# Layer 1's attention entry with its casts shared over three engines, wide matmuls of ones at the kernel's entry, and a moved order in layer 0's attention

## The chip, the cores and the metric

The kernel runs on one core of a Trainium2 chip. A core has a matrix engine (TensorE, PE in the profile; its weight loads are listed apart as PEld), three engines that work on tiles element by element (VectorE or DVE, ScalarE or ACT, GpSimd or POOL) and a queue that issues most transfers (SyncE or SP). Each engine runs its own instructions strictly in order and waits for others by semaphores. The metric is the device time of one execution in microseconds, and the number to predict is its median over the runs.

## The reference, cut to what matters

The model has two layers over 1024 tokens of width 1024, all in float32. Layer 0 mixes tokens by differential attention (8 heads), layer 1 by latent attention (16 heads) with a rotary key that all heads share. Each is followed by a gated MLP with a short convolution.

```python
# layer 1's attention (mla_attention)
proj = h @ w_in
c_q = rms_norm(proj[..., :384], q_norm_g)
c_kv = rms_norm(proj[..., 384:640], kv_norm_g)
k_pe = apply_rope(proj[..., 640:], cos, sin)          # one rotary key of 32 for all heads
q = (c_q @ w_uq).reshape(b, s, 16, 64 + 32)
kv = (c_kv @ w_ukv).reshape(b, s, 16, 64 + 64)
sc = (einsum('bqhd,bkhd->bhqk', qn, k_nope) + einsum('bqhr,bkr->bhqk', qp, k_pe)) * scale
p = masked_softmax(sc, mask)                          # chunk-causal
o = einsum('bhqk,bkhe->bqhe', p, v)
```

## The kernel before, in words

Products run in a rounded float32 format. To keep float32 accuracy, an operand is split into a high part (a cast, helper `hi`, L123 to L127) and a low part (the difference, helper `lo`, L129), and a product is made of three matmuls (`mm3`, L116 to L121: high by low, high by high, low by high). So every tile that enters a product costs one cast, on ACT unless the call names DVE, and one subtraction, on DVE unless the call names POOL. PSUM, where products land, is divided into two big tiles S of 1024 columns, three banks b and one bank u of 512.

**The entry** (`diff_attention`, from L373). Rows of x are loaded, squared on ACT (L157), scaled by the root on DVE (norm, L440), transposed on PE (L448), cast and subtracted, and then multiplied by the first weights. The order on PE, DVE, ACT and POOL is written out by hand in the string `FIRST` (L366). In it T are the transposes of a row tile, H and L its casts and low parts, Q, R and N the squares, the root and the norm, G the copy of the gains out of PSUM, p the products of the first weights, and z0 to z3 runs of `spin` (L191): matmuls of a tile of ones that nobody reads. Their counts are 0, 28, 0 and 6, each 128 columns wide.

**Layer 0's attention** runs in steps of two blocks of queries, four steps to a head. What each step emits on the four engines is written by hand in `DA_SCORE` (L324), one row for each step of a head, and `DA_SECOND` for the very second step. Tokens without a mark belong to the current step, one more apostrophe is one step older, a plus one step ahead. S are scores on PE, M the maximum on DVE, E the exponential on ACT, I the inverse sum on DVE, C the scaling (POOL in a head's first two steps), X the mixing of the two maps on DVE, T transposes on PE, H and L their cast and low part, A the product with the values, O the copy of the output. Q, R, N and F finish a head's half: Q3 is a low part of the squares on POOL, F (L1947, L1948) adds them up on PE. U and V are the next projections (0 and 1 on PE), W the next weight's cast (h, ACT) and low part (l, POOL). Engines take only their own tokens, so two neighbouring tokens of different engines may change places without any change to an engine's order.

**Layer 1's attention** (`mla_input` L1526, `mla_heads` L1650) isn't ordered by hand. Instructions are emitted in program order, and a planner with its own estimates of their lengths places them on the engines. While `mla_input` still makes the latents, the first steps of the attention start (`early`). A head has four steps t, and a step scores two blocks of queries (L1977 to L1991: products into S, maximum on DVE, exponential on ACT). Beside them, `prepare(t)` and `units(t)` (L1749 on) feed the next pair of heads:

- `rotary` (L1737) writes the rotary key into head 0's key tile, 32 rows by ACT and 32 by DVE; `share(j, half)` (L1744) copies it into the key tiles of heads 1 to 3, casts of 64x1024 on ACT. Heads 2 and 3 get theirs in steps 3 to 6.
- `split_w(p)` and `split_v(p)` cast the weights and the values of a pair on ACT and subtract on POOL.
- `q_unit` makes half a head's queries: nine matmuls, a multiplication by the table on DVE (L1694), a cast on ACT, a low part on DVE for heads 0 and 1 and on POOL after.
- `k_unit` makes half a pair's keys: six matmuls, two casts of 64x512 on ACT, two low parts on DVE.
- The six units of pair 1 are due in steps 2, 3, 4, 5, 6 and 7.

Of the kernel before, what the change touches and what calls it, by code (L numbers as in the profile page):

```python
# [10 lines left out]
F32 = mybir.dt.float32  # L11
F32R = mybir.dt.float32r
# [6 lines left out]
P = 128  # L19
S = 1024  # L20
# [36 lines left out]
class Trunk:  # L57
# [133 lines left out]
    def spin(self, n):  # L191

        ps = self.bank("u")
        for _ in range(n):
            self.nc.tensor.matmul(ps[:, :P], self.ones, self.ones, start=True, stop=True)

    def gain(self, place, src):
        g = self.at(place, [P, src.shape[-1]])
# [4 lines left out]
    def constants(self):  # L203
        nc, a = self.nc, self.a
        c = lambda name, shape, dt=F32: self.const.tile(shape, dt, name=name, tag=name)
        self.ident = c("ident", [P, P])
        make_identity(nc, self.ident)
        self.row = self.at("u13", [8, P])
        nc.scalar.dma_start(self.row, a["attn_norm_g"][0:1, :].rearrange("o (k p) -> (o k) p", p=P))
        nc.scalar.preload_act_table_set("natural_log_exp_and_others")  # L210
        self.mhalf = c("mhalf", [P, 1])
        nc.gpsimd.memset(self.mhalf, -0.5)
        self.eps = c("eps", [P, 1])
        nc.gpsimd.memset(self.eps, EPS)
        self.ones = c("ones", [P, P], F32R)
        nc.vector.tensor_scalar(self.ones, self.ident, 0.0, 1.0, ALU.mult, ALU.add)
        self.conv = [c(f"conv{l}", [P, 2 * NF, 4]) for l in range(2)]
        self.g_sub = c("g_sub", [P, 1])
        self.neglam = c("neglam", [P, 1])
# [69 lines left out]
    def steps(self, attend, units, prepare, n, apart=False):  # L289
# [32 lines left out]


    DA_SCORE = (  # L324
# [4 lines left out]
    )  # L329

    DA_SECOND = "S0 I1' Vc' Ukd' T3'' H2'' M0 L2'' A1'' C0' X0' H3'' E0b L3'' Wh U0 A2'' E0a Vt' N3'''' A3'' C1' O'' Wl' X1' Q2'' I0 U1 C0 S1 X0 Us Vh' Q1'' T0' H0' Q3'' Up F'' Um M1 Ua Wl R1'' Vl' E1b V0 E1a L0' I1 A0' R2'' R3'' Uqa Uqd Uqe Uqb C1 X1 N1'' Uqc V1 T1 T0 Uqf H0"

    DA_END = (
# [9 lines left out]
    def da_steps(self, attend, units, prepare, n, extra):  # L343
# [4 lines left out]
        with self.tc.manual_schedule(engines={E.PE, E.DVE, E.Activation, E.Pool}):  # L348
            for t in range(-1, first + len(self.DA_END)):
                while len(steps) < min(n, t + 2):  # L350
# [3 lines left out]
                    for name, u in zip("UV", units(x)):  # L354
                        steps[x].parts.update({name + part: f for part, f in u.items()})
                row = self.DA_SECOND if t == 1 else self.DA_SCORE[t % 4] if t < first else self.DA_END[t - first]
                for name in row.split():
# [15 lines left out]
    def diff_attention(self, o_d, project):  # L373
        nc, a = self.nc, self.a
# [6 lines left out]
            k=self.ring("u0", "u1", "u2"), qh=self.ring("u3", "u4"), v=self.ring("u5", "u6", "u7"),  # L381
            P=self.ring("u8", "u9", "u10", "u11", "u12"), pT=self.ring("u13", "u14", "u15"),
# [11 lines left out]
        def fetch_w(h, which):  # L394
            if h < DA_HEADS:
                raws[h, which] = self.fetch(a["da_wqkv"][h, which], D)
# [24 lines left out]
        x, r = [], {}  # L421
# [10 lines left out]
        def fetch_tab(half):  # L432
            s = slice(half * 512, half * 512 + 512)
            nc.sync.dma_start(tab[:, :, s], a["rope_da"][:, :, s])
# [82 lines left out]
            next(ends[which], None)  # L517

        todo = dict(c=column, g=spreads, G=keep, t1=lambda: fetch_tab(1), f1=lambda: fetch_w(1, 1), s=self.load_constants)
        for i, n in enumerate((0, 28, 0, 6)):  # L520
            todo[f"z{i}"] = lambda n=n: self.spin(n)
        for i in range(NT):
            todo.update({f"{z}{i}": lambda f=f, i=i: f(i) for z, f in zip("QRNX", (squares, root, norm, fetch_x))})
# [1002 lines left out]
    def mla_input(self, W, hts, turns, v_d, heads_of):  # L1526
# [120 lines left out]
                heads.early()  # L1647
        return heads

    def mla_heads(self, cT, v_d, o_d):  # L1650
        nc, a = self.nc, self.a
        pairs = MLA_HEADS // 2
        heads = [dict() for _ in range(MLA_HEADS)]
        W, V, raws = {}, {}, {}
        w_places = [("u2", "u3"), ("u4", "u5")]
        v_ring, q_ring, t_ring = self.ring("s13", "s4"), self.ring("s1", "s11", "s5", "s9"), self.ring("h10", "h11", "h8")
        k_places, kT = ["s0", "s10", "s12", "s8"], []
# [3 lines left out]
            P=self.ring("u12", "u6", "u7", "u8", "u9"), pT=self.ring("u0", "u1", "u10", "u11"), o=self.ring("h4", "h5", "h6", "h7"),  # L1661
        )

        def fetch_w(p):
            raws["w"] = self.fetch(a["mla_w"][p], D)

        def split_w(p):
            raw = raws["w"]
            W[p] = [self.at(x, [P, D], F32R) for x in (w_places[p % 2] if p else self.cut("s9"))]
            self.hi(W[p][0], raw)  # L1670
            self.lo(W[p][1], raw, W[p][0], nc.gpsimd)

        def fetch_v(p):
# [2 lines left out]
        def split_v(p):  # L1676
            rv = raws["v"].rearrange("p (k h e) -> p k h e", h=2, e=64)
            V[p] = v = v_ring([P, NT, 2, 2, 64], F32R)
            self.hi(v[:, :, :, 0, :], rv)
            self.lo(v[:, :, :, 1, :], rv, v[:, :, :, 0, :], nc.gpsimd)  # L1680

        def q_unit(h, half):
            if half == 0:
                heads[h]["q"] = q_ring([P, 2, S], F32R)
            q = heads[h]["q"]
            acc = self.bank()
            off = (h % 2) * 384
            for k in range(3):
                wh, wl = (w[:, off + k * P : off + (k + 1) * P] for w in W[h // 2])
                self.mm3(acc, wh, wl, cT.q(0, half, k), cT.q(1, half, k), k == 0, k == 2)  # L1690
            yield
            s = slice(half * 512, (half + 1) * 512)
            t = t_ring([P, 512])
            nc.vector.tensor_mul(t, acc, cs[:, s])  # L1694
            self.hi(q[:, 0, s], t)
            self.lo(q[:, 1, s], t, q[:, 0, s], nc.gpsimd if h > 1 else None)

        def k_unit(p, half):
            acc = self.bank()
            for k in range(2):  # L1700
                wh, wl = (w[:, 768 + k * P : 768 + (k + 1) * P] for w in W[p])
                self.mm3(acc, wh, wl, cT.kv(0, half, k), cT.kv(1, half, k), k == 0, k == 1)
            yield
            s = slice(half * 512, (half + 1) * 512)
            for j in range(2):
                k = heads[2 * p + j]["k"] = kT[(2 * p + j) % 4]
                src = acc[j * 64 : j * 64 + 64]
                self.hi(k[0:64, 0, s], src)
                self.lo(k[0:64, 1, s], src, k[0:64, 0, s])

        def pair_units(p):
            return [
                lambda: k_unit(p, 0), lambda: k_unit(p, 1),
                lambda: q_unit(2 * p, 0), lambda: q_unit(2 * p, 1),
                lambda: q_unit(2 * p + 1, 0), lambda: q_unit(2 * p + 1, 1),
            ]

        fetch_w(0)
        split_w(0)

        def first(*which):
# [12 lines left out]
        def k_tiles(n):  # L1734
            kT.extend(self.at(place, [P, 2, S], F32R) for place in k_places[len(kT) : n])

        def rotary(half, t):  # L1737

            k_tiles(1)
            s = slice(half * 512, (half + 1) * 512)  # L1740
            for x, r0 in enumerate((64, 96)):
                self.hi(kT[0][r0 : r0 + 32, :, s], t, nc.vector if x else None)

        def share(j, half):  # L1744
            k_tiles(j + 1)
            s = slice(half * 512, (half + 1) * 512)
            self.hi(kT[j][64:128, :, s], kT[0][64:128, :, s])

        def prepare(t):  # L1749
            p, u = divmod(t, 8)  # L1750
            if t == 0:
                fetch_w(1)
            if t == 1:
                split_w(1)
                k_tiles(4)
            if 3 <= t < 7:
                share(2 + (t - 3) // 2, (t - 3) % 2)
            for at, ahead, f in ((2, 1, fetch_v), (4, 1, split_v), (5, 2, fetch_w), (7, 2, split_w)):
                if u == at and p + ahead < pairs:
                    f(p + ahead)  # L1760
            if t >= 4 * MLA_HEADS - 10:
                prefetch[0]()

        def units(t):
            p, u = divmod(t, 8)
            if t == 0:
                return [u() for u in pair_units(0)[1::2]]

            at = (2, 3, 4, 5, 6, 7) if p == 0 else (0, 1, 3, 4, 5, 7)
            return [pair_units(p + 1)[i]() for i in range(6) if at[i] == u and p + 1 < pairs]  # L1770

        def attend(t):
# [533 lines left out]
```

## Time and profile before

| | |
|---|---|
| median of 3 runs | 2388.96 us (2388.56 to 2390.82) |
| the profiled execution | 2391.28 us, of which 2389.5 us are the profile's span |
| mean granted TensorE clock | 0.997 |
| HBM traffic | 158.85 MB read, 52.43 MB written, 88 GB/s over the span |
| DMA share in the first fortieth of the span | 0.4 of 16 engines |

The profile is that of one execution. Times count in microseconds from the span's start. A row of the order of time has start, length, engine, line, operation and tiles (out<-in), shapes and count, and in brackets the idle time of the engine before it and what ended it. A group's row has the count, the busy time, the mean of one in ns, and the idle time before. Matmuls overlap in a pipeline, so the length of one row is longer than the pace at which they follow each other.

### The profile page before, as it was taken

How to read it: one execution, taken by the hardware profiler on the slowest of the kernel's cores; microseconds unless marked ns; L12 is line 12 of the kernel's file. 1: busy time of each engine (PE TensorE's matmuls, PEld its weight loads, DVE VectorE, ACT ScalarE, POOL GpSimd, SP SyncE). 2: the span in 40 equal slices, each digit the busy share in tenths (PEclk: the TensorE clock that was granted, in tenths of full speed). 3: DMA queues.
4: the chain of work that ended last, by engine and by line, in shares of the span. 5: the costliest groups of instructions: out<-in, count | busy, mean ns of one | idle time of the engine just before them, and what ended most of it. 6: DMA issues, size and time to landing. Idle time of an engine off the chain costs nothing.

```text
span 2389.5 us, 32702 instructions
## 1 busy us (share of the span) xinstructions
PE 2351.9 (98%) x11979; PEld 2003.0 (84%) x11979; DVE 1926.9 (81%) x3180; ACT 1291.6 (54%) x2367; POOL 611.2 (26%) x485
## 2 busy tenths in 40 slices
PE   9999999999999999999999999999999999999998
PEld 8888888888888888888898889988888888887886
DVE  6788888758888888899854778886488888888997
ACT  5677777745444444354445777775354444443544
POOL 4555555324000000000132666664320000000001
PEclk9999999999999999999999999999999999999999
DMA  4111111332222222642221211123322222227502
GB/s 147 40 36 36 48 37 54 111 114 102 89 89 80 80 86 82 233 168 90 86 95 56 63 38 41 41 95 107 115 71 90 87 80 80 89 80 282 176 1 79
DMA packets 95664, 213.39 MB, mean 89 GB/s; under 512 B 8712, under 2 KB 33936, under 8 KB 95504
## 3 DMA queue, kind: packets, MB, share of 16 engines
q1 hardware_dynamic: 86304, 183.51, 23.3%
q10 hardware_dynamic: 9200, 27.80, 3.1%
q8 instruction: 94, 1.54, 0.3%
q14 instruction: 66, 0.54, 0.1%
HBM read 158.85 MB, written 52.43 MB: 88 GB/s over the span
## 4 chain that ended last, share of the span: by engine, by line
PE 86%; DVE 6%; ACT 2%; DMA 2%; POOL 2%; issue 2%; SPq 0%; POOLq 0%; DVEq 0%; ACTq 0%
PE S L119 13%; PE S L121 13%; PE S L120 13%; PE b L119 8%; PE b L121 8%; PE b L120 8%; PE u L119 4%; PE u L121 4%; PE u L120 4%; PE b L260 2%; PE u L2012 1%; PE u L2011 1%; PE S L1856 1%; PE S L1855 1%; PE b L1902 1%
## 5 line engine op out<-in xcount | busy, mean ns | idle before, releaser
L167 POOL TENSOR_TENSOR st<-st,mhalf 128x1 f32<-128x1 f32 x56 | 35.5, 634 | 1305.4 <-DVE st L164 1301.4
L119 PE MATMUL S<-s,u 128*128 128x512 f32 (+1 forms) x800 | 302.1, 378 | 2.4 <-DVE s L130 2.0
L121 PE MATMUL S<-s,u 128*128 128x512 f32 (+1 forms) x800 | 301.1, 376 | 0.4 <-DVE u L130 0.4
L120 PE MATMUL S<-s,u 128*128 128x512 f32 (+1 forms) x800 | 301.0, 376 | 0.0
L127 ACT CAST u<-h 128x512 fp32r<-128x512 f32 (+2 forms) x242 | 145.5, 618 | 272.9 <-DVE h L1023 271.4
L119 PE MATMUL b<-s,u 128*128 128x512 f32 x588 | 230.9, 393 | 2.0 <-DVE u L130 1.4
L121 PE MATMUL b<-s,u 128*128 128x512 f32 x588 | 229.0, 390 | 0.0
L120 PE MATMUL b<-s,u 128*128 128x512 f32 x588 | 229.0, 390 | 0.0
L1080 DVE SCALAR_TENSOR_TENSOR u<-u,conv,u 128x1023 f32<-128x1023 f32 (+1 forms) x176 | 225.0, 1278 | 0.8 <-ACT u L1076 0.7
L149 POOL TENSOR_TENSOR u<-u,st 128x512 f32<-128x512 f32 (+7 forms) x160 | 169.0, 1066 | 164.9 <-DVE st L1997 103.7
L127 ACT CAST s<-u 128x512 fp32r<-128x512 f32 (+3 forms) x230 | 145.4, 665 | 94.8 <-PE u L121 27.1
L119 PEld LDWEIGHTS S<-s,u 128*128 128x128 f32 x800 | 150.5, 188 | 30.7 <-DVE s L130 2.6
L130 DVE TENSOR_TENSOR u<-b,u 128x512 fp32r<-128x512 f32 (+1 forms) x256 | 158.8, 631 | 20.7 <-ACT u L127 18.2
L127 ACT CAST u<-b 128x512 fp32r<-128x512 f32 (+1 forms) x256 | 135.0, 547 | 74.9 <-PE b L1902 42.2
L121 PEld LDWEIGHTS S<-s,u 128*128 128x128 f32 x800 | 150.5, 188 | 28.1 <-DVE u L130 0.6
L120 PEld LDWEIGHTS S<-s,u 128*128 128x128 f32 x800 | 150.5, 188 | 27.4
L119 PE MATMUL u<-s,s 128*128 128x512 f32 (+1 forms) x408 | 162.4, 398 | 1.4 <-DVE h L602 0.6
L121 PE MATMUL u<-s,s 128*128 128x512 f32 (+1 forms) x408 | 158.0, 387 | 0.0
L120 PE MATMUL u<-s,s 128*128 128x512 f32 (+1 forms) x408 | 157.6, 386 | 0.0
L130 DVE TENSOR_TENSOR s<-u,s 128x512 fp32r<-128x512 f32 (+2 forms) x204 | 139.0, 714 | 11.9 <-ACT s L127 11.6
L1083 ACT ACTIVATE u<-u 128x1024 f32<-128x1024 f32 x44 | 46.7, 1062 | 187.2 <-DVE u L1080 187.2
L130 DVE TENSOR_TENSOR u<-h,u 128x512 fp32r<-128x512 f32 x171 | 117.5, 687 | 32.5 <-ACT u L127 31.5
(289 smaller groups left out, 6533.4 us busy)
## 6 DMA issues: line engine op xcount, KB each, us to landing
u<-in_ffn_up SPq DMA_DIRECT2D x88, 512.0 KB, 3.8
g_d<-u ACTq DMA_DIRECT2D x44, 512.0 KB, 2.6
u<-in_ffn_down SPq DMA_DIRECT2D x66, 256.0 KB, 4.7
u<-g_d SPq DMA_DIRECT2D x62, 256.0 KB, 4.3
s<-in_da_wqkv SPq DMA_DIRECT2D x23, 512.0 KB, 3.8
x_d<-u SPq DMA_DIRECT2D x16, 512.0 KB, 2.9
s<-x_d SPq DMA_DIRECT2D x8, 1024.0 KB, 9.9
u<-o_d SPq DMA_DIRECT2D x24, 256.0 KB, 2.9
```

The lines of the kernel that those rows point to most:

```text
L119: mm(out, lh, rl, start=first, stop=False, skip_group_check=onto)
L120: mm(out, lh, rh, start=False, stop=False, skip_group_check=onto)
L121: mm(out, ll, rh, start=False, stop=last, skip_group_check=onto)
L127: self.nc.scalar.copy(out, src)
L130: (eng or self.nc.vector).tensor_sub(out, src, hi.bitcast(F32))
L149: self.nc.gpsimd.tensor_mul(x, x, s.to_broadcast(list(x.shape)))
L167: nc.gpsimd.tensor_tensor(r, s, self.mhalf, ALU.pow)
L260: self.nc.tensor.transpose(ps[:, j * P : (j + 1) * P], probs[t][:, k : k + P], self.ident)
L1080: nc.vector.scalar_tensor_tensor(t[half][:, back:], u[half][:, : S - back], w, t[half][:, back:], ALU.mult, ALU.add)
L1083: nc.scalar.activation(t[0], t[0], AF.Silu)
L1855: nc.tensor.matmul(sc[c][:, b : b + m], ql[c][:, qs], kt[:, c, :m], start=True, stop=False)
L1856: nc.tensor.matmul(sc[c][:, b : b + m], qh[:, c, qs], kt[:, c, :m], start=False, stop=True)
```

## The change

Three places change.

1. `spin` multiplies the ones by a tile `wide` of 512 columns, which four ACT copies of the 128x128 ones fill at the start. The counts fall from 28 to 7 and from 6 to 2.
2. Tokens move in `DA_SCORE` and `DA_SECOND`. Per engine: T3 of the step before goes from behind the next row's S0 to the end of row 0 on PE, and T2 goes ahead of V1; on ACT E0b goes ahead of H1 and E0a behind it in row 0, E0a ahead of Wh in row 1, and Uqa ahead of R2; on DVE M0 goes ahead of Ukd, I0 ahead of X1, and N1 ahead of X1 at the end of the row; on POOL Wl goes ahead of C1. The two tokens moved in row 2 and the two in row 3 belong to different engines.
3. Engines of layer 1's entry are spelled out by letters (S for ACT, V for DVE, P for POOL). Against before, these differ: to DVE go the casts of weight pair 1, of value pair 2, of the shares (2, second half) and (3, first half), of query half 3 and of key piece 3; to POOL go the low parts of query halves 1 and 2, and to DVE that of query half 6. The share (3, first half) is emitted in step 10 in place of 5. The units of pair 1 are due in steps 2, 2, 3, 5, 5 and 7.

```diff
-            self.nc.tensor.matmul(ps[:, :P], self.ones, self.ones, start=True, stop=True)
+            self.nc.tensor.matmul(ps, self.ones, self.wide, start=True, stop=True)
...
+        self.wide = self.at("h4", [P, 512], F32R)
+        for j in range(4):
+            nc.scalar.copy(self.wide[:, j * P : (j + 1) * P], self.ones.bitcast(F32))
...
     DA_SCORE = (
-        "S0 S1 M0 Up O'' R2''' X1' R3''' V0 N1''' M1 T1' Ua E0a H1' L1' Uka E1a T0' H0' Ukb V1 Ukc E0b T2' L0' I0 E1b A0' N2'''",
-        "S0 I1' Vc' Ukd' T3'' H2'' M0 L2'' A1'' C0' X0' H3'' E0b L3'' Wh U0 A2'' E0a Vt' N3'''' A3'' C1' O'' Wl' X1' Q2'' I0 U1 C0 S1 X0 Us Vh' Wl Q1'' T0' H0' Q3'' Up F'' Um M1 Ua R1'' Vl' E1b V0 E1a L0' I1 A0' R2'' R3'' Uqa Uqd Uqe Uqb C1 X1 N1'' Uqc V1 T1 T0 Uqf H0",
+        "S0 S1 M0 Up O'' R2''' V0 X1' R3''' E0b N1''' M1 T1' Ua H1' E0a L1' Uka E1a T0' H0' T2' Ukb Ukc L0' I0 E1b V1 A0' N2''' T3'",
+        "S0 I1' Vc' H2'' M0 Ukd' L2'' A1'' C0' X0' H3'' E0b L3'' U0 E0a A2'' Wh Vt' N3'''' A3'' O'' Wl' Q2'' C1' I0 X1' U1 C0 S1 X0 Us Vh' Wl Q1'' T0' H0' Q3'' Up F'' Um M1 Ua R1'' Vl' E1b V0 E1a L0' I1 A0' Uqa R2'' R3'' Uqd Uqb C1 N1'' Uqe X1 Uqc V1 T1 T0 Uqf H0",
...
-        for i, n in enumerate((0, 28, 0, 6)):
+        for i, n in enumerate((0, 7, 0, 2)):
...
+    SHARES = "SSSVVS"
+    SHARED_AT = (3, 4, 10, 6)
+    ROTARY = "SV"
+    VALUES = "SSVSSSSS"
+    WEIGHTS = "SVSSSSSS"
+    QUERIES = "SSSVSSSSSSSSSSSSSSSSSSSSSSSSSSSS"
+    QUERIES_LOW = "VPPVPPVPPPPPPPPPPPPPPPPPPPPPPPPP"
+    KEYS = "SSSVSSSSSSSSSSSSSSSSSSSSSSSSSSSS"
+    UNITS_AT = (2, 2, 3, 5, 5, 7)
...
+        eng = lambda x: {"S": None, "V": nc.vector, "P": nc.gpsimd}[x]
...
-            self.hi(W[p][0], raw)
+            self.hi(W[p][0], raw, eng(self.WEIGHTS[p]))
...
-            self.hi(v[:, :, :, 0, :], rv)
+            self.hi(v[:, :, :, 0, :], rv, eng(self.VALUES[p]))
...
-            self.hi(q[:, 0, s], t)
-            self.lo(q[:, 1, s], t, q[:, 0, s], nc.gpsimd if h > 1 else None)
+            self.hi(q[:, 0, s], t, eng(self.QUERIES[2 * h + half]))
+            self.lo(q[:, 1, s], t, q[:, 0, s], eng(self.QUERIES_LOW[2 * h + half]))
...
-                self.hi(k[0:64, 0, s], src)
+                self.hi(k[0:64, 0, s], src, eng(self.KEYS[4 * p + 2 * half + j]))
...
-            self.hi(kT[j][64:128, :, s], kT[0][64:128, :, s])
+            self.hi(kT[j][64:128, :, s], kT[0][64:128, :, s], eng(self.SHARES[2 * j + half - 2]))
...
-            if 3 <= t < 7:
-                share(2 + (t - 3) // 2, (t - 3) % 2)
+            for n, at in enumerate(self.SHARED_AT):
+                if at == t:
+                    share(2 + n // 2, n % 2)
...
-            at = (2, 3, 4, 5, 6, 7) if p == 0 else (0, 1, 3, 4, 5, 7)
+            at = self.UNITS_AT if p == 0 else (0, 1, 3, 4, 5, 7)
```

`DA_SECOND` changes as row 1 does.

More of the change, by code (lines that the diff above doesn't have):

```diff
@@ L324 @@
     DA_SCORE = (
[4 rows of a table removed]
[4 rows of a table added]
     )
-    DA_SECOND = "S0 I1' Vc' Ukd' T3'' H2'' M0 L2'' A1'' C0' X0' H3'' E0b L3'' Wh U0 A2'' E0a Vt' N3'''' A3'' C1' O'' Wl' X1' Q2'' I0 U1 C0 S1 X0 Us Vh' Q1'' T0' H0' Q3'' Up F'' Um M1 Ua Wl R1'' Vl' E1b V0 E1a L0' I1 A0' R2'' R3'' Uqa Uqd Uqe Uqb C1 X1 N1'' Uqc V1 T1 T0 Uqf H0"
+    DA_SECOND = "S0 I1' Vc' H2'' M0 Ukd' L2'' A1'' C0' X0' H3'' E0b L3'' U0 E0a A2'' Wh Vt' N3'''' A3'' O'' Wl' Q2'' C1' I0 X1' U1 C0 S1 X0 Us Vh' Q1'' T0' H0' Q3'' Up F'' Um M1 Ua Wl R1'' Vl' E1b V0 E1a L0' I1 A0' Uqa R2'' R3'' Uqd Uqb C1 N1'' Uqe X1 Uqc V1 T1 T0 Uqf H0"
     DA_END = (
@@ L1741, in rotary @@
             for x, r0 in enumerate((64, 96)):
-                self.hi(kT[0][r0 : r0 + 32, :, s], t, nc.vector if x else None)
+                self.hi(kT[0][r0 : r0 + 32, :, s], t, eng(self.ROTARY[x]))
         def share(j, half):
```

4 rows, old and new, of the table DA_SCORE are left out of this document.

## The prediction

> **What bounds the kernel now.** I read the page first, then the stretches stage by stage, then the order of time inside the stages that the diff touches, and last TensorE's waits.
>
> ```profile
> span 2389.5 us, 32702 instructions
> PE 2351.9 (98%) x11979; PEld 2003.0 (84%) x11979; DVE 1926.9 (81%) x3180; ACT 1291.6 (54%) x2367; POOL 611.2 (26%) x485
> PE 86%; DVE 6%; ACT 2%; DMA 2%; POOL 2%; issue 2%; SPq 0%; POOLq 0%; DVEq 0%; ACTq 0%
> ```
>
> TensorE (PE) is busy 2351.9 of 2389.5 us, so all the idle time there is to win in the whole kernel is 37.6 us. None of the three edits takes a product out of the layers: each can only fill idle time, or shorten a stretch at a low clock. So I ask where the 37.6 us lie.
>
> ```profile
> 0.00:25.00 25.00, 21.21 (x131) 20.70 (x132) 13.11 (x21) 15.22 (x24) 8.88 (x18) 1.00 0.81 291
> 47.10:52.60 5.50, 5.50 (x24) 4.56 (x25) 3.52 (x11) 3.09 (x10) 2.86 (x4) 1.00 0.01 1
> 85.00:200.00 115.00, 114.91 (x633) 98.91 (x631) 94.99 (x172) 85.91 (x169) 62.53 (x44) 1.00 0.11 37
> 1315.00:1320.00 5.00, 5.00 (x29) 4.20 (x28) 3.69 (x8) 4.90 (x7) 1.11 (x1) 1.00 0.58 148
> 1320.00:1330.00 10.00, 5.76 (x28) 4.08 (x28) 7.57 (x18) 8.82 (x18) 6.95 (x4) 0.97 0.44 150
> 1329.00:1334.00 5.00, 5.00 (x27) 4.68 (x28) 3.58 (x14) 3.13 (x8) 5.00 (x4) 0.66 0.44 123
> 1355.00:1380.00 25.00, 23.92 (x156) 21.16 (x154) 21.64 (x53) 19.54 (x44) 17.02 (x14) 1.00 0.17 54
> 1380.00:1595.00 215.00, 214.50 (x1405) 193.81 (x1404) 177.51 (x432) 164.77 (x361) 139.81 (x114) 1.00 0.15 43
> ```
>
> The columns are the stretch, its length, the busy time of PE, its weight loads, DVE, ACT and POOL with their counts, then the granted clock. The entry is open (21.21 of 25). Layer 0's attention is shut: 0.09 us idle in 115. Layer 1's attention is open for ten microseconds (5.76 of 10 at 1320 to 1330) and shut again from 1380 on (0.5 idle in 215). One price for later: 24 matmuls of 512 columns fill 5.50 us, 0.229 us each at full clock.
>
> **Part 1, the entry.**
>
> ```profile
> 1.34 1.28 ACT L210 ACT_TABLE_LOAD   x1 [1.34 <-PEq L2296]
> 3.68 1.97 PE L506 MATMUL S<-ident,h 128*128 128x128 f32 x8 [0.26 <-DVE h L501]
> 4.68 1.06 ACT L157 ACTIVATE u<-u 128x1024 f32<-128x1024 f32 x1 [2.05 <-DMA u<-in_x]
> 5.30 6.21 PE L195 MATMUL u<-ones 128*128 128x128 f32 x28
> 7.32 2.47 DVE L440 SCALAR_TENSOR_TENSOR u<-u,st,S 128x1024 f32<-128x1024 f32 x2
> 11.31 3.63 PE L448 MATMUL b<-ident,u 128*128 128x128 f32 x16
> 12.42 0.59 ACT L127 CAST s<-b 128x512 fp32r<-128x512 f32 x1 [4.12 <-PE b L448]
> 13.76 1.02 ACT L510 COPY s<-S 128x1024 f32<-128x1024 f32 x1
> 14.60 1.24 PE L195 MATMUL u<-ones 128*128 128x128 f32 x6
> 16.14 0.36 PE L119 MATMUL u<-s,s 128*128 128x256 f32 x1 [0.30 <-DVE s L130]
> 19.18 1.03 PE L448 MATMUL b<-ident,u 128*128 128x128 f32 x8
> 1310.39 0.27 ACT L127 CAST s<-u 128x128 fp32r<-128x128 f32 x1
> ```
>
> The 28 matmuls of ones hold PE from 5.30 to 11.31, 0.215 us each. The clock column reads 1.00 here, yet the transposes of L448 take 3.63/16 = 0.227 us each at 11.31 and 1.03/8 = 0.129 at 19.18: PE runs at about half pace until about 15 us, and the column doesn't know it. The normalised tiles of x are there far earlier: the two DVE passes end at 7.32 + 2.47 = 9.79, the first at about 8.6. So the first transposes wait some 2.7 us for the ones alone.
>
> Seven matmuls of 512 columns cost 7 x 0.229 = 1.6 us at full and 3.2 us at half pace. They end between 6.9 and 8.5, either way before 8.6. The transposes then start at 8.6 in place of 11.31, and behind them ACT's casts (idle 4.12 us before 12.42, waiting for these very transposes), the copy of the gains and the first real product at 16.14 move with them: **-2.7 us**. PE is nearly full from 16.14 to 25, so the shift stays. If the clock rises before the transposes, the first cast starts still earlier, by 4 transposes x (0.227 - 0.129) = 0.4 us, and the second, held by ACT, by no more than that again; the upper end is -3.5. The last two ones at 14.60 take at most 2 x 0.46 = 0.9 in place of 1.24 and stand beside the casts: nothing.
>
> Cost of making the wide tile: four ACT copies, bounded by the 0.27 us cast of 128x128, 1.1 us in all. ACT is free from 1.34 + 1.28 = 2.62 until x lands at 4.68, 2.06 us, so they are hidden; without that cover they would delay the squares by 1.1 and the gain would be 1.6.
>
> The Trainium skill, "TensorE: Matmul & The Clock Gate", section "Part 4: PE-mode transpose", says that transposes don't count as activity for the clock; its Part 1 asks for about 3.4 us of sustained work. By that rule the shorter run of ones never fills such a window and the first products would run at half pace. The trace leans the other way, since after 6.2 us of ones the pace was still half, and it rose after 3.3 us of transposes. The result by the rule is the first rival.
>
> **Part 2, the order of layer 0's attention.** Only two moves change an engine's own order in earnest: the transposes T3 of the step before go ahead of the scores S0 on PE, and on DVE the maximum M0 goes ahead of the key's low part (Ukd). With them POOL does a weight's low part before C1, and DVE does I0 before X1. No instruction is added or dropped. What can be won is the wait for the total F:
>
> ```profile
> 161.40 0.97 DVE L611 SCALAR_TENSOR_TENSOR u<-h,u 64x512 fp32r<-64x512 f32 x1
> 161.52 0.49 PE L1902 MATMUL b<-ident,u 128*128 128x128 f32 x3
> 165.83 0.47 DVE L1894 SCALAR_TENSOR_TENSOR u<-u,st 128x256 f32<-128x256 f32 x1
> 166.23 0.15 DVE L1886 RECIPROCAL st<-st 128x2 f32<-128x2 f32 x1
> 167.31 2.41 POOL L130 TENSOR_TENSOR s<-s,s 128x1024 fp32r<-128x1024 f32 x1
> 169.69 1.60 POOL L130 TENSOR_TENSOR h<-h,h 128x512 fp32r<-128x512 f32 x1
> 171.35 0.50 PE L1947 MATMUL b<-h,ones 128*128 128x512 f32 x1
> ```
>
> F starts at 171.35, when POOL's chain I0 (166.23), C0, weight low, square low ends at 171.29. I0 ahead of X1 brings the chain forward by 0.47; M0 ahead of Ukd makes DVE wait for scores that now stand behind T3 (0.49 at most), and puts them back. I take **0**. The bounds per head pass are -0.1 (85 to 200 holds no more than 0.09 us idle) and +0.5, in the six passes that run this row with an F in it -0.6 to +3.
>
> **Part 3, the entry of layer 1's attention.**
>
> ```profile
> PE S L119 <- ACT u L1991: 4.2, 4, 1.4
> L127 ACT CAST s<-s 64x1024 fp32r<-64x1024 f32 x3 | 2.9, 1041 | 0.0
> L127 ACT CAST s<-b 64x512 fp32r<-64x512 f32 x4 | 2.3, 582 | 0.1
> 1305.00:1315.00 10.00, 10.00 (x50) 8.31 (x50) 7.68 (x15) 6.62 (x16) 8.42 (x6) 1.00 0.25 82
> 1307.99 2.39 POOL L130 TENSOR_TENSOR u<-u,u 128x1024 fp32r<-128x1024 f32 x1
> 1313.16 1.28 POOL L130 TENSOR_TENSOR u<-h,u 32x512 fp32r<-32x512 f32 x1 [0.73 <-ACT u L127]
> 1313.63 1.35 DVE L130 TENSOR_TENSOR s<-h,s 128x512 fp32r<-128x512 f32 x1 [0.70 <-ACT s L127]
> 1315.09 0.69 DVE L125 CAST s<-u 32x1024 fp32r<-32x1024 f32 x1
> 1317.39 0.42 PE L119 MATMUL S<-s,s 128*128 128x384 f32 x1
> 1334.48 0.40 PE L119 MATMUL b<-s,u 128*128 128x512 f32 x1
> ```
>
> Four times PE's scores wait for an exponential on ACT, 4.2 us together, between 1315 and 1330, where ACT is busy 4.90 + 8.82 of 15 us. Three shares of the rotary keys (2.9 us) stand in that queue. Terms:
> - One of the three (head 2, second half) goes to DVE: 2.9/3 = 0.97 us off ACT's queue, so all four waits together end that much sooner: -0.97. On DVE it costs some 0.69 by the cast of L125, and DVE is busy 7.57 of 10: hidden.
> - The second query product (nine matmuls, 9 x 0.229 = 2.06 us, now at 1334.48) is due one step earlier and falls where PE waits: -2.06. Its cast still loads ACT, by about the 0.58 of a key's cast: +0.58.
> - The weight cast, one key cast and one query cast that leave ACT lie before 1315, where ACT has 3.4 of 10 us free: some 2.2 us of work, of which I let 0.2 reach the queue.
> - The waits let the clock fall: 0.66 over 1329 to 1334 is 5 x 0.34/0.5 = 3.4 us at half pace, 1.7 lost. I take half of that back, -0.85, since the idle time that does it is about halved.
>
> Sum 0.97 + 2.06 - 0.58 + 0.2 + 0.85 = **3.5 us gained**. The top end is the waits and the half pace together, 4.2 + 1.7 = 5.9. On the other side stand two low parts moved to POOL (about 1.28 each, the 2.39 of a weight's low part ahead of them) and the third head's share, deferred to step 10. The rotary chain and the scores at 1317.39 pass over POOL: a delay of 2 x 1.28 there, less the relief of 0.97, is a loss of 1.6. So part 3 lies between -5.9 and +1.6.
>
> DVE's low part at 1313.63 took 1.35 us while POOL's ran to 1314.44, so moved casts can be held by POOL. The Trainium skill, "SBUF — State Buffer", section "SBUF: two separate sides", calls that an exclusive lock; by it a cast that starts behind a weight's low part could wait the whole of it, and part 3 would keep about 1.1 of its 3.5. No run here shows a DVE copy in that place.
>
> **Sum.** -2.7 + 0 - 3.5 = -6.2. The profiled execution took 2391.28 us (2389.5 of span and 1.78 around it), so 2385.1 like for like; the median is 2.32 below it, and 2388.96 - 6.2 = **2382.8 us**.
>
> **Rivals.**
> - **The clock stays at half behind the shorter ones.** The 24 first products of 256 columns would start at 13.4 and take 6.0 us in place of 3.0 (16.14 to 19.18): 2388.96 - 2.7 + 3.0 - 3.5 = 2385.8. For it: 6 us of ones didn't raise the pace. Against: those were narrow, a weight load for each; transposes did.
> - **Both gains in full**: -3.5 - 5.9, 2379.6. For it: ACT is the only thing that the four waits name. Against: the stream of casts on ACT loses one share only.
> - **The waits stay, with another engine at their end**: DVE at 21.64 of 25 in 1355 to 1380 is as full as ACT was. Part 3 gives nothing, 2386.3.
> - **Slower: the waits of 1355 to 1380 go on.** That stretch has 1.08 us of PE idle in 25, and the later pairs 0.5 in 215, in an order that a planner makes from its own estimates. If casts on DVE and the deferred share put pair after pair in the crowded order, 250 us cost 250 x 1.08/25 = 10.8; with part 1 that is 2388.96 - 2.7 + 10.8 = 2397.1. It decides from 2.7 us on, a quarter of that density. Against: from the third pair on nothing is assigned otherwise.
>
> **How the numbers follow.** The forecast has 0.50, the clock rival 0.14, both in full 0.16, the waits that stay 0.10, slower 0.10. About 0.2% of the time, 4.8 us, is what a measurement can tell from no change, so faster means under 2384.2: most of the forecast (0.46) and all of the full gain, with 0.02 of the rest, 0.64. Within the bound lie 0.04 of the forecast and 0.22 of the two rivals, 0.26. Slower 0.10. The range, 2379.0 to 2389.0, takes in all but the slower rival and the far end of the full gain, and the +3 of part 2 and +1.6 of part 3 added one at a time.
>
> **What would show it.** The first L448 transposes at 8.6 and the first L119 at about 13.4; L448 at 0.13 us each by then would put the clock right. PE idle at the total F unchanged at some 0.06. In layer 1, two casts of 64x1024 in a row on ACT, waits for L1991 under 2.5 us, no stretch at 0.5. The prediction is wrong if the first L119 stays at 16, if the waits return under DVE's or POOL's name, or if 1380 to 1595 loses more than a microsecond.

## The result, and the profile after

| | median | runs |
|---|---|---|
| before | 2389.64 us | 10, 2388.56 to 2393.01 |
| changed | 2384.74 us | 10, 2382.59 to 2389.33 |

The ratio is 0.998, with a 95% interval of 0.9971 to 0.9988: 4.9 us faster by the medians. The profiled execution took 2383.38 us, 7.9 less than that of before, and part of those 7.9 us is no effect of the change (below). Two executions of the experiments further down stand apart by their granted clock: one of e5's ran at 0.535 and took 4390.09 us, which its ratio leaves out, and one of e10's ran at 0.945 and took 2403.63 us, which e10's ratio contains.

The page of the changed kernel has the span, the busy times and the shares of the chain of waits:

```profile
span 2381.6 us, 32686 instructions
PE 2344.1 (98%) x11954; PEld 1994.6 (84%) x11954; DVE 1931.5 (81%) x3185; ACT 1288.2 (54%) x2365; POOL 613.7 (26%) x486
PE 86%; DVE 6%; DMA 2%; POOL 2%; issue 2%; ACT 1%; SPq 0%; POOLq 0%; DVEq 0%; ACTq 0%
```

TensorE's idle time hardly moved, 37.5 us for 37.6, while its busy time fell by 7.8. So on balance the gain is work that TensorE no longer does (ones) or does at full pace: the idle time that was filled in layer 1 stands again at the entry, where TensorE now waits for the tile in place of spinning, and in layer 0. The stages show where, with the columns of before; the later ones are shifted by what the kernel has gained until then.

```profile
0.00:25.00 25.00, 19.69 (x138) 17.74 (x139) 16.10 (x24) 17.83 (x32) 9.43 (x19) 1.00 0.87 328
81.20:196.20 115.00, 114.20 (x627) 98.30 (x626) 95.07 (x172) 85.46 (x168) 62.85 (x44) 1.00 0.11 37
1301.00:1311.00 10.00, 8.80 (x44) 7.14 (x42) 9.06 (x16) 3.92 (x12) 9.39 (x7) 1.00 0.29 92
1311.00:1321.00 10.00, 9.90 (x51) 8.22 (x52) 8.64 (x17) 9.34 (x16) 4.21 (x4) 1.00 0.47 159
1321.00:1331.00 10.00, 8.62 (x57) 6.72 (x55) 8.72 (x23) 8.89 (x21) 10.00 (x8) 1.00 0.37 119
1329.00:1334.00 5.00, 5.00 (x35) 4.43 (x35) 3.83 (x14) 3.28 (x10) 3.44 (x5) 1.00 0.11 45
1347.50:1372.50 25.00, 24.55 (x161) 22.05 (x160) 22.65 (x55) 19.41 (x45) 17.16 (x14) 1.00 0.17 54
1372.50:1587.50 215.00, 214.52 (x1406) 193.90 (x1405) 178.26 (x435) 164.94 (x361) 140.64 (x114) 1.00 0.15 44
```

Layer 0's attention got worse: 0.80 us idle in 115, where it had 0.09. Layer 1's entry got better: 1.20 + 0.10 + 1.38 = 2.68 idle from 1301 to 1331, where 1320 to 1330 alone had 4.24, no stretch at a lowered clock behind it, 0.45 idle where there was 1.08, and nothing lost in the long tail (0.48 in 215).

The order of time in the entry of the changed kernel:

```profile
2.65 0.89 ACT L219 CAST h<-ones 128x128 fp32r<-128x128 f32 x4
5.18 2.39 PE L195 MATMUL u<-h,ones 128*128 128x512 f32 x7
8.35 1.85 PE L451 MATMUL b<-ident,u 128*128 128x128 f32 x12 [0.78 <-DVE u L443]
...
12.40 0.36 PE L119 MATMUL u<-s,s 128*128 128x256 f32 x1 [0.86 <-DVE s L130]
```

The first transposes start at 8.35 in place of 11.31, now behind the normalised tile and not behind the ones. They run at 1.85/12 = 0.154 us, waits between them included, where they took 0.227, and the first product stands at 12.40 in place of 16.14: 3.74 us.

The waits of TensorE in two stretches, the group for the total F in layer 0 (60 to 425; first the row of before, then that of the changed kernel) and the one for the exponentials in layer 1's entry (1290 to 1345, the changed kernel), with us in total, times and longest:

```profile
PE b L1947 <- POOL h L130: 1.5, 2, 0.9
...
PE b L1963 <- POOL h L130: 2.3, 6, 0.4
...
PE S L119 <- ACT u L2007: 1.3, 1, 1.3
```

F (L1947 before, L1963 now) waits 0.38 us in each of six head passes, where it had waited in two of them. The scores wait for an exponential once, not four times.

**What varies by itself.** Each profile has a stretch at half clock where layer 0's attention ends, and its length differs between the profiles. First before, then the changed kernel. The third row is the same changed kernel run again (e8), at another place:

```profile
446.00:456.00 10.00, 7.59 (x29) 6.29 (x29) 7.23 (x15) 8.26 (x18) 7.15 (x7) 0.66 0.35 117
```

```profile
445.00:451.00 6.00, 4.56 (x19) 3.74 (x20) 3.33 (x5) 4.70 (x9) 4.48 (x5) 0.72 0.07 23
```

```profile
1019.00:1026.00 7.00, 6.15 (x20) 4.92 (x21) 7.00 (x13) 4.25 (x9) 0.00 (x0) 0.76 1.00 376
```

A granted clock of 0.66 over 10 us is 10 x 0.34/0.5 = 6.8 us at half pace, 3.4 lost; 0.72 over 6 us is 3.4 us, 1.7 lost. The same kernel run again had the short one too, and from 1021 on 7 x 0.24/0.5 = 3.4 us of it besides, 1.7 lost, where the first profile had none. Its profiled execution took 2388.07 us, 4.7 more than the first one, and 1.7 is only a part of that. So a span taken once is uncertain by several us, and below an effect counts where a landmark or a wait shows it and the median doesn't contradict.

### The profile page after: what moved, and what is told of

It reads as the page before. It is cut to its first block, busy times and chain, and to the rows that moved or that the text cites. A ratio compares the mean times of both kernels' runs of the same rounds, so it can differ in the third digit from the quotient of the medians.

```text
span 2381.6 us, 32686 instructions
## 1 busy us (share of the span) xinstructions
PE 2344.1 (98%) x11954; PEld 1994.6 (84%) x11954; DVE 1931.5 (81%) x3185; ACT 1288.2 (54%) x2365; POOL 613.7 (26%) x486
## 4 chain that ended last, share of the span: by engine, by line
PE 86%; DVE 6%; DMA 2%; POOL 2%; issue 2%; ACT 1%; SPq 0%; POOLq 0%; DVEq 0%; ACTq 0%
PE S L119 13%; PE S L121 13%; PE S L120 13%; PE b L119 8%; PE b L121 8%; PE b L120 8%; PE u L119 4%; PE u L121 4%; PE u L120 4%; PE b L263 2%; PE u L2028 2%; PE u L2027 1%; PE S L1872 1%; PE S L1871 1%; PE b L1918 1%
## 5 line engine op out<-in xcount | busy, mean ns | idle before, releaser
L127 ACT CAST s<-u 128x512 fp32r<-128x512 f32 (+3 forms) x229 | 144.4, 664 | 93.7 <-PE u L121 26.4
```

The lines of the kernel that those rows point to most:

```text
L127: self.nc.scalar.copy(out, src)
```

## The experiments

All were timed in five rounds against the kernel before on the same chip. e1 to e4 shared one chip, e5 to e8 a second and e9 to e12 a third, where the kernel before had medians of 2389.65, 2389.11 and 2390.39 us; between these groups the ratios compare better than the medians. The ratio stands with its 95% interval.

| run | median | ratio |
|---|---|---|
| e1 wide ones alone | 2386.02 | 0.9985 (0.9976 to 0.9994) |
| e2 order alone | 2393.05 | 1.0013 (1.0005 to 1.0022) |
| e3 layer 1's entry alone | 2385.54 | 0.9984 (0.9975 to 0.9993) |
| e4 changed, old order | 2383.68 | 0.9975 (0.9966 to 0.9983) |
| e5 key's low part ahead of M0 again | 2388.79 | 0.9999 (0.999 to 1.0008) |
| e6 half as many narrow ones | 2388.19 | 0.9994 (0.9986 to 1.0003) |
| e7 no ones | 2387.40 | 0.999 (0.9981 to 0.9999) |
| e8 changed kernel again | 2383.99 | 0.9977 (0.9968 to 0.9986) |
| e9 due steps alone | 2389.13 | 0.9994 (0.9986 to 1.0003) |
| e10 engines and shares alone | 2388.93 | 1.0003 (0.9991 to 1.0014) |
| e11 changed, T3 behind S0 again | 2380.85 | 0.9959 (0.9947 to 0.9971) |
| e12 old order, a query cast on ACT | 2381.13 | 0.9961 (0.9949 to 0.9973) |

### The three parts, one at a time

The first four put each part by itself on the kernel before, and then leave the order out of the changed kernel. e1 takes part 1 of the change, e2 part 2, e3 part 3, e4 parts 1 and 3.

> The kernel before with the wide ones alone (7 and 2 matmuls of 512 columns). Theory, read from the two traces: the whole gain of the entry, 3.7 us, comes with it: the first product of layer 0 at 12.4 us in place of 16.1, time 2389.6 - 3.7 = 2385.9, and the waits for the total F as before (two of them, 1.5 us). Rival, my prediction's own size: 2.7 us, first product at 13.4. Rival, the shift is eaten by loads or by the ACT queue before 60 us: within 1 us of before.

> The kernel before with the moved tokens of layer 0's attention alone. Theory: the move costs time; six waits for the total F of about 0.4 us, 2.3 us in all, in place of two of 1.5, and 0.4 us more in every one of six head passes: 2390 to 2392. Rival: the order is neutral by itself and the six waits in the changed kernel come from the shifted entry: waits as before, 2389.6.

> The kernel before with the new engines and due steps of layer 1's entry alone. Theory: 4.8 us gained between 1290 and 1380: the four waits for the exponential (4.2 us) shrink to one of about 1.3, the stretch at half clock at 1329 disappears, 2384.8. Rival, my prediction's size: 3.5 us, 2386.1. Rival: the gain needs the earlier start, under 2 us.

> The changed kernel with layer 0's order as it was before. Theory: both gains add and the cost of the order is gone: 2389.6 - 3.7 - 4.8 = 2381.1, some 2 to 3 us faster than the changed kernel (2384.7); the waits for the total F fall back to 0.1 to 0.2 us each. Rival (the order is neutral): 2384.7, as the changed kernel.

By the ratios, each uncertain by about 2 us, e1 gives -3.6, e2 +3.1 and e3 -3.8 us. In e1 the first product stands at 12.92. In e2 and in every kernel with the new order unaltered F waits in all six passes. What the order costs is read from F itself: the row of its line, duration min/median/max in ns, and the start of the first and the last. Between the first and the 13th lie six heads. One row each of before, the changed kernel and e4:

```profile
L1947 PE MATMUL b<-h,ones x13: 398/398/502, 96.4 to 426.8; 128*128 128x512 f32 x13
```

```profile
L1963 PE MATMUL b<-h,ones x13: 398/399/502, 92.6 to 424.0; 128*128 128x512 f32 x13
```

```profile
L1963 PE MATMUL b<-h,ones x13: 398/398/504, 92.9 to 421.8; 128*128 128x512 f32 x13
```

The six heads take 331.4 us with the new order (e2, from 96.5 to 427.9, as well as the changed kernel) and 328.9 with the old one (e4). Before they took 330.4, but that profile holds two longer waits at F, 1.5 us together, which e4 doesn't have; 330.4 - 1.5 = 328.9 agrees. So behind the new entry the order costs 331.4 - 328.9 = 2.5 us, 0.4 a head. Beside the old entry it costs 331.4 - 330.4 = 1.0: the old order has longer waits at F in all four profiles with the old entry (before, e3, e9, e10: 0.5 to 1.8 us) and none in e1, e4 and e12, which have the wide ones. So e1's expectation of two waits as before failed, part 1 gains at F besides, and of e2's +3.1 only 1.0 is located. e4 should have gained 2.5 on the changed kernel and by the medians gained 1.1 (0.3 against e8), which the intervals don't tell from nothing. Its profile has the long half-clock stretch (6.8 us at 443) where the changed kernel's has the short one, which takes 1.7 back in the profile; the runs don't say whether the kernel or chance sets the length. e4's own forecast of 2381.1 was missed by 2.6.

### What makes the wide ones work

> The kernel before with half the narrow ones (14 and 3 of 128 columns): 14 x 0.215 = 3.0 us, as long as seven wide ones at half clock. Theory: what the wide ones add beside being shorter is the clock: here the transposes start at 8.4 as well but run at 0.21 us each, the clock rises only after 12 us, the first product comes at 13.3 to 13.6, 2387.0. Rival, length alone: first product at 12.4 to 12.9 and 2386.0, as with the wide ones.

> The wide ones alone, with all their counts at zero. Theory: the transposes can't start before the norm at 8.3 anyway, and run at half pace; first product at 13.3 to 13.6 and part of the first products at half clock: 2386.5 to 2389. Rival, the ones are of no use: 2386.0, as with the wide ones.

```diff
-        for i, n in enumerate((0, 28, 0, 6)):
+        for i, n in enumerate((0, 14, 0, 3)):      # e6, narrow ones
...
-        for i, n in enumerate((0, 7, 0, 2)):
+        for i, n in enumerate((0, 0, 0, 0)):       # e7, on e1
```

The order of time in e6:

```profile
5.37 3.23 PE L195 MATMUL u<-ones 128*128 128x128 f32 x14
8.54 3.62 PE L448 MATMUL b<-ident,u 128*128 128x128 f32 x16
...
13.40 0.36 PE L119 MATMUL u<-s,s 128*128 128x256 f32 x1 [0.96 <-DVE s L130]
```

In e7:

```profile
8.72 3.67 PE L451 MATMUL b<-ident,u 128*128 128x128 f32 x16 [2.91 <-DVE u L443]
13.50 0.58 PE L119 MATMUL u<-s,s 128*128 128x256 f32 x1 [1.10 <-DVE s L130]
13.88 0.42 PE L120 MATMUL u<-s,s 128*128 128x256 f32 x1
```

And in e1:

```profile
5.09 3.33 PE L195 MATMUL u<-h,ones 128*128 128x512 f32 x7
8.63 1.85 PE L451 MATMUL b<-ident,u 128*128 128x128 f32 x12 [0.21 <-DVE u L443]
12.92 0.36 PE L119 MATMUL u<-s,s 128*128 128x256 f32 x1 [0.85 <-DVE s L130]
```

All three start the transposes at 8.5 to 8.7. Behind 14 narrow ones, as long as the wide run, they take 3.62/16 = 0.226 us each, half pace, and the first product stands at 13.40. Without any ones they take 0.229, and the products behind them start at half pace too. Behind seven wide ones they run at 0.154, and the first product comes half a microsecond earlier. All seven profiles with the wide ones have their first twelve transposes at 0.154 to 0.177, all six with narrow ones at 0.226 to 0.227, so this is no accident of one execution. Ending the ones early gives 16.14 - 13.40 = 2.74, and the width the rest, 0.5 in e1 and 1.0 in the changed kernel (0.25 to 1.0 over the seven). It is still there at the start of the first F, in the old order: 96.4 before, 93.7 in e6, 93.2 in e1 and 95.3 in e7, where the first products lost time at half pace. So even no ones at all were better here than 28 narrow ones. e6's time shows less, 0.9 by the median, with an interval from 3.3 gained to 0.7 lost; its forecast of 2387.0 was missed by 1.2.

The Trainium skill, "TensorE: Matmul & The Clock Gate", "Part 4: PE-mode transpose", has it that transposes don't count as activity for the clock. e7 is in line with it, since 3.67 us of them left the next products at half pace. Part 1 of the same page of the Trainium skill says that some 3.4 us of sustained work release the clock and that how much runs slow depends on where a free-running window falls. That the seven wide ones took 2.39 us in one profile and 3.33 in another is in line with the second half. The narrow ones don't agree with a plain reading of the first: 6.21 us of them before left the transposes at half pace.

### Why the new order waits, and which token does it

> The changed kernel with one pair of DVE tokens back in its old order: the key's low part Ukd ahead of the maximum M0. Theory: DVE's wait for scores that stand behind T3 (1.1 us idle) is what makes POOL's chain to the total F late; with Ukd in that gap the six waits fall from 0.4 to under 0.1 us and some 2.5 us come back: 2382 to 2383. Rival: T3 ahead of S0 delays the chain by itself, or the swap of C1 and the weight's low part on POOL does: the waits stay at 0.4, 2384.7.

> The changed kernel itself beside the three others on the same chip: 2384.7, six waits for the total F of 0.4 us.

> The changed kernel with T3 back behind the scores S0, all other moves kept. The theory of the run before (the maximum ahead of the low part) has fallen; new theory: the low part in front collides with POOL's weight low part (2.83 us in place of 0.97), and what makes the total F late in the changed order is two things, S0 some 0.25 us later behind T3, and X1 on DVE beside POOL's next weight (2.59 in place of 2.40). So the distance from F to F falls by 0.2 to 0.25 us a head, from 20.50 to about 20.3, the wait for F to 0.15. Rival, S0 alone: 20.1 and no wait. Rival, POOL's own order alone: 20.5 and 0.4.

In both, `DA_SECOND` changes alike.

```diff
-S0 I1' Vc' H2'' M0 Ukd' L2''
+S0 I1' Vc' Ukd' H2'' M0 L2''           (e5)
...
-A0' N2''' T3'",
+A0' N2'''",
-S0 I1' Vc' H2'' M0
+S0 I1' Vc' T3'' H2'' M0                (e11, S0 ahead of T3 again)
```

In order of time, the head pass of the changed kernel that answers to the rows of before:

```profile
158.77 0.17 DVE L1881 MEMSET S<- 64x128 f32 x1 [1.12 <-PE S L1872]
159.95 1.10 DVE L614 SCALAR_TENSOR_TENSOR u<-h,u 64x512 fp32r<-64x512 f32 x1
163.08 0.16 DVE L1902 RECIPROCAL st<-st 128x2 f32<-128x2 f32 x1
163.41 3.77 DVE L1910 SCALAR_TENSOR_TENSOR u<-u,st 128x256 f32<-128x256 f32 x2
164.17 2.59 POOL L130 TENSOR_TENSOR s<-s,s 128x1024 fp32r<-128x1024 f32 x1
166.72 1.60 POOL L130 TENSOR_TENSOR h<-h,h 128x512 fp32r<-128x512 f32 x1
168.37 0.50 PE L1963 MATMUL b<-h,ones 128*128 128x512 f32 x1 [0.38 <-POOL h L130]
```

And of e11:

```profile
158.68 0.17 DVE L1881 MEMSET S<- 64x128 f32 x1 [0.78 <-PE S L1872]
...
159.87 0.88 DVE L614 SCALAR_TENSOR_TENSOR u<-h,u 64x512 fp32r<-64x512 f32 x1
...
166.40 1.62 POOL L130 TENSOR_TENSOR h<-h,h 128x512 fp32r<-128x512 f32 x1
```

In the changed kernel, with S0 behind T3, DVE has nothing to do for 1.12 us before M0 (its memset, L1881): the maximum was moved ahead of the key's low part, so no other work stands there. With S0 first again it is idle for 0.78, 0.34 less, the key's low part behind it takes 0.88 in place of 1.10, and F waits for nothing (the waits of e11 have no row for it):

```profile
L1963 PE MATMUL b<-h,ones x13: 398/398/503, 93.5 to 421.5; 128*128 128x512 f32 x13
```

Six heads take 328.0 us in e11: 3.4 less than changed and 0.9 less than the old order. Its forecast, 0.15 of wait left and 20.3 us between the two Fs of a head, was too cautious: no wait is left and the distance is 19.96, so its rival, S0 alone (20.1 and no wait), came nearer. The one token accounts for the whole loss, and with it back the other moves gain 0.9/6 = 0.15 a head. e11 beats both kernels: its ratio of 0.9959 stands against 0.9980 and 0.9977 (e8) of the changed kernel, 4 to 5 us, of which F shows 3.4.

e5 takes back the other half of the conflict and fails. With the key's low part ahead of M0 again F still waits, six heads take 334.9 us, 3.5 more than changed, and a second wait comes up:

```profile
158.73 2.40 POOL L130 TENSOR_TENSOR s<-s,s 128x1024 fp32r<-128x1024 f32 x1
158.85 2.83 DVE L614 SCALAR_TENSOR_TENSOR u<-h,u 64x512 fp32r<-64x512 f32 x1
161.70 0.17 DVE L1881 MEMSET S<- 64x128 f32 x1
```

```profile
PE b L1963 <- POOL h L130: 2.5, 6, 0.4
PE b L119 <- DVE u L130: 2.0, 6, 0.4
```

The low part (L614) takes 2.83 us where it took 0.97 before and 1.10 in the changed kernel. It begins 0.12 us behind the weight's low part on POOL, which the moved token Wl had put there, and ends 0.55 behind it. The theory, that the order of M0 and Ukd alone set the wait, fell. By these rows the moves of Wl and M0 belong together; no run moves Wl back alone.

### Which half of part 3 gives the gain

> The kernel before with the new due steps of pair 1's units alone, every engine as before. My prediction gave the earlier query product 2.06 of its 3.5 us. Theory by the traces: the products fill the waits, but ACT keeps its three shares and gets the casts sooner: 1 to 2 us gained, 2388, waits for the exponential 2 to 3 us in 1300 to 1345. Rival, engines matter alone: waits 4.2 us as before, 2389.5. Rival, due steps do it all: waits 1.3 us, 2385.5.

> The kernel before with the new engines and the deferred share alone, the due steps as before. Theory: one share less and the upstream casts gone from ACT shorten the four waits by 2 to 3 us: 2386.5 to 2387.5. Rival, my prediction's price (one share, 0.97 us): 2388.5. Rival, engines do it all: waits 1.3 us, 2385.5.

> The changed kernel with layer 0's old order, and the cast of query half 3 back on ACT, where it was before the change. Theory: on DVE this cast takes 2.5 us beside POOL's low parts in place of some 0.6, the maximum stands behind it, ACT idles 2.9 us and PE waits 1.3 to 1.4 us for the exponential that follows; on ACT it lies in that idle time. The wait goes: 1.3 us faster than the same kernel with the cast on DVE (2383.7), 2382.4, the fastest of all. Rival, the next thing on DVE is late by the same: 2383.7.

```diff
-    UNITS_AT = (2, 3, 4, 5, 6, 7)
+    UNITS_AT = (2, 2, 3, 5, 5, 7)          # e9: this alone; e10: all but this
...
-    QUERIES = "SSSVSSSSSSSSSSSSSSSSSSSSSSSSSSSS"
+    QUERIES = "SSSSSSSSSSSSSSSSSSSSSSSSSSSSSSSS"     # e12, on e4
```

Waits of TensorE between 1290 and 1345. In e9:

```profile
PE S L119 <- ACT u L2004: 1.6, 2, 1.4
PE b L260 <- DVE s L130: 0.9, 1, 0.9
```

In e10:

```profile
PE S L119 <- ACT u L2004: 4.2, 4, 1.4
```

And the same 65 us in three kernels, before, e10 and e12:

```profile
1280.00:1345.00 65.00, 59.73 (x322) 50.98 (x321) 39.70 (x94) 42.15 (x94) 29.08 (x24) 0.97 0.25 76
```

```profile
1280.00:1345.00 65.00, 59.85 (x330) 50.96 (x329) 45.02 (x103) 40.17 (x94) 34.71 (x28) 1.00 0.26 78
```

```profile
1280.00:1345.00 65.00, 64.09 (x356) 53.90 (x355) 46.30 (x106) 43.49 (x97) 37.08 (x30) 1.00 0.25 78
```

The stretch is the same in time, not in work: at its start e12 is some 4 us ahead of before. Engines and shares alone (e10) take 2 us off ACT's 42.15 and leave the four waits at 4.2 and the idle time at 65 - 59.85 = 5.15, against 5.27. The forecast for e10, waits shorter by 2 to 3 us, failed. Due steps alone (e9) cut the waits for ACT to 1.6 and bring one for DVE instead; the idle time is 65 - 60.65 = 4.35. Both medians are within what can be told from before. Together (e3) they leave 2.82 idle and gain 3.8 us. So the idle time falls by 0.92 and 0.12 alone and by 2.45 together, an interaction: with free engines but no product due TensorE still waits, and with a product due but ACT loaded it waits for the next operand.

The one wait of 1.3 us that is left in the changed kernel has its cause on DVE:

```profile
1307.20 1.39 POOL L149 TENSOR_TENSOR u<-u,st 128x512 f32<-128x512 f32 x2
1307.59 2.53 DVE L125 CAST s<-h 128x512 fp32r<-128x512 f32 x1
1308.56 1.27 POOL L130 TENSOR_TENSOR u<-h,u 32x512 fp32r<-32x512 f32 x1
1310.49 0.47 ACT L2007 ACTIVATE u<-S,st 128x256 f32<-128x256 f32 x1 [2.93 <-DVE st L2006]
1311.10 0.50 PE L119 MATMUL S<-s,s 128*128 128x512 f32 x1 [1.31 <-ACT u L2007]
```

The cast of query half 3, moved to DVE, takes 2.53 us beside POOL, which is busy from 1307.20 to 1308.56 + 1.27 = 1309.83 (a cast twice as wide, 128x1024, took 0.69 on DVE when it began at 1303.05, at the end of a POOL operation); the maximum for the next exponential (L2006, 0.41 us at 1310.04) stands behind it, and ACT is idle for 2.93 meanwhile. Put back on ACT in e12 it takes 0.62, the wait is gone and 0.91 us of the 65 are idle. From e4 to e12 the transposes that start at 1218.34 and 1602.71 in e4 move up by 0.59 and 2.09, so the entry gains 1.5, where 1.3 was expected. The times show more, 2.55 by the medians and 3.3 by the ratios, but come from two chips and the intervals overlap. e12, too, beats both kernels by its ratio. e11 and e12 together weren't run.

## Why the prediction was right, point by point, and where its steps failed

The forecast was 2382.8 us in a range of 2379.0 to 2389.0; the median is 2384.74. Sign and mechanism held for two parts, and the order in layer 0 is the step that failed.

- **Part 1: the mechanism was right and the term too small.** -2.7 was predicted with -3.5 as its upper end; the first product moved by 3.74, beyond that end (3.22 in e1's profile), and e1 gained 3.6. The step that was mis-sized is the pace of the transposes, which the sum left at half and allowed 0.8 for. The -2.7 by itself is what e6 shows (13.40). The rival of the clock at half didn't come: the 24 first products run at full pace in the changed kernel, in e1 and in e6, and at half for the first four microseconds only where no ones stand at all (e7). The copies of the wide tile were hidden, as said: 0.89 us from 2.65 to 3.54, with x's squares starting at 4.39.
- **Part 2: the step that failed.** "I0 ahead of X1 brings the chain forward by 0.47; M0 ahead of Ukd [...] puts them back. I take 0". The balance was off by 0.4 a head: behind the new entry the cost was 2.5 us, inside the bound of +3, and no row had shown that the two cancel. What was missing: DVE's idle 1.12 us before M0 comes from two moves together: one puts the scores back on PE, and the other takes away the work that DVE had to fill such a gap. e11 takes the first back alone, and the wait is gone. The gain of 0.47 was also smaller than written, as the weight's low part on POOL took 2.59 us where it took 2.41, beside the mixings on DVE that now span 3.77; from I0 to F went 5.29 us (163.08 to 168.37) after 5.12.
- **Part 3: the total was right, its split wrong.** -3.5 was predicted and e3 gained 3.8. But 0.97 for a share off ACT's queue and 2.06 for the earlier product were added as if each stood alone. Alone, neither gave its term: e10 left the four waits unaltered at 4.2, and e9's idle time fell by 0.9 (5.27 to 4.35), not 2.06. Together they took 2.45 off the idle time in e3, where the terms without the clock make 2.65. The warning in the same part held: a DVE copy beside POOL does stretch, 2.53 us against 0.69 for the rows that the price of a cast was taken from. The Trainium skill's rule in "SBUF — State Buffer", "SBUF: two separate sides", is that of a port which the one of DVE and POOL that starts first holds for its whole instruction. The 2.83 row agrees, where the low part ends 0.55 us behind one POOL operation; in the 2.53 row the cast outlasts three POOL operations in a row, where the rule names one. The sum that was made by it, 1.1 of 3.5 kept, was too low: 3.8 was left, and the cast beside POOL costs 1.3 by the wait and 1.5 by the transposes in e12.
- **The half pace** at 1329 was to be half gone (0.85); in the changed kernel, e3 and e4 it doesn't appear, in e1, e2, e6 and e7, which keep the old entry of layer 1, it does. So it gave more than its term, 1.7. But that the waits let the clock fall doesn't hold by itself: e10 keeps all four waits, 4.2 us, and its clock stays at 1.00 (in e9, too). What sets it is open.
- **The rivals.** "The waits stay, with another engine at their end" is what e9 shows in small (0.9 for DVE); in the changed kernel the wait that names ACT is in truth DVE's. "Slower: the waits go on" isn't seen: 1372.5 to 1587.5 has 0.48 idle in 215.
- **The sum.** By the ratios the parts alone give -3.6 + 3.1 - 3.8 = -4.3, and the change 4.8. Predicted was 6.2. That this came within 2 us is partly luck: part 1 gained about 0.9 more than its term and the order cost 2.5 by F in place of nothing, two errors that partly cancel. Without the order e4 gained 6.0; the intervals of e4 and of the change overlap, so the cost of the order rests on F and not on these times.

Not settled: the profiled run is 4.19 us ahead at 526 and only 2.73 at 1219, in stages that the change doesn't touch. e1 shows nearly the same (4.03 and 2.83), e11 doesn't (5.45 and 5.25). These are the starts of the same transposes, read in both profiles. Most of the loss is waits of TensorE, mainly between 540 and 570 and at 1019: all its waits of at least 0.15 us from 520 to 1025 make 3.45 us before, 4.69 in the changed kernel, 4.49 in e1 and 3.39 in e11. The largest is one for a low part on DVE at 1018.81, 1.40 us in the changed kernel, 0.62 before and 0.43 in e11. Why it grows is open.

## What to carry to other kernels

When two moves touch the same gap, one that makes an operand later and one that removes the work which covered its lateness, their sum isn't the sum of the two: look at what the waiting engine has left to do. Price an operation on DVE by a row that stands beside POOL at that place, not by the mean of its kind. And where work is spread and also asked for earlier, try each half by itself before crediting either: here neither alone gained what the times can tell from nothing.

## What the runs showed of the hardware that was not expected

- A cast and a two-input operation on DVE took 2.53 and 2.83 us beside POOL, where a wider cast (128x1024), begun at the end of a POOL operation, took 0.69 in the same run and the same low part 0.97 before.
- 6.2 us of matmuls of 128 columns left TensorE at half pace (0.227 us a transpose behind them); seven matmuls of 512 columns, 2.4 to 3.3 us of work, were followed by transposes at 0.154 to 0.177, waits included. Each matmul has a weight load of its own in both, so the columns for each load differ.
- The half-clock stretch at the end of layer 0's attention lasts 3.4 or 6.8 us in the profiles, and the changed kernel had one more of 3.4 us at 1021 in one of its two profiles. Each 3.4 us costs 1.7 us of the time.
